# Reversed values copied in halves, key roots transposed later, one home for the triangular inverses of an RWKV-7 layer

## The chip, the cores and the metric

The kernel is one launch on one core of a Trainium2 chip. The metric is the device time of an execution in microseconds (us). A core has TensorE (PE, matrix products; its weight loads are shown as PEld), VectorE (DVE), ScalarE (ACT), GpSimd (POOL) and SyncE (SP, which issues nearly all DMAs here), which run their own instruction queues and wait for each other by semaphores. 16 DMA engines move data between DRAM and the on-chip memory (SBUF), and from DRAM to DRAM.

## The reference: one step of a four-layer backbone

The model has four layers over 640 tokens (128 of a context, 512 of a latent grid) and 1024 channels: retention, RWKV-7 time mixing, differential attention and neighbourhood attention. Each layer is a modulated norm, a mixer and an output product added to the residual stream. The change lies in the RWKV-7 layer and in what borders on it. Cut to what is computed there, for `x` the normed input:

```python
xx = centred_shift(h) - h
x_r, x_w, x_k, x_v, x_a, x_g = [h + xx * mu[n] for n in range(6)]
r, k, v, g = (x_r, x_k, x_v, x_g) @ w_in                 # 1024 x 4096
kk = k * k_k
kk = kk * rsqrt(max(sum(kk * kk, -1), 1e-12))            # per token and head of 64
for dr in range(2):                                      # forward, backward
    wlog  = -softplus(-(w0[dr] + tanh(x_w @ wA[dr]) @ wB[dr])) - 0.5
    decay = exp(-exp(wlog))
    a     = sigmoid(a0[dr] + (x_a @ aA[dr]) @ aB[dr])
    kd    = k * (1 + (a - 1) * k_a)
    seq   = (r, decay, kd, v, kk, a)                     # dr == 1: flipped in time
    # per token: s = s * decay + (s @ -kk) (kk * a)^T + v kd^T ;  y = s @ r
o = (head_layer_norm(y_f + y_b) + bonuses) * silu(g)
return o @ w_out
```

## The kernel before

**Numbers.** A product of two float32 matrices is made of three matmuls of rounded halves (lines 88, 89 and 90: high by high, low by high, high by low). ScalarE casts the high part (line 96 or 170), VectorE or GpSimd subtracts it for the low part (line 93). Weights come in pieces `wr` of 512 KB (line 160).

**Who sets the order.** The program is written with tiles that are taken from pools. A list scheduler with a timeline of its own orders the instructions of each engine by priority (`high_priority` raises it), and then lays the tiles out. A pool that is opened when another is closed gets the same addresses, so the first write to a tile waits until the last use of whatever lay there before. SyncE issues DMAs in one queue: a DMA that waits holds up all behind it.

**Stages.** Retention runs to about 586 us. Transition 0 is its output product (`ret_w_out`, 16 loads `wr`, matmuls `oa`), the residual, the norm of the next layer and its modulation (`w_mod`, matmuls `pm` on line 326); its rows of retention's output come back from DRAM as `oraw`. Then `rwkv_project` runs to about 1190, `rwkv_mix` to 1590, then transition 1 (`rwkv_w_out`) and the two attention layers.

**rwkv_project** mixes the shifted input (`wxh`, `wxl`: the parts of the mixed input `wm`) and projects it in the order k, the two low-rank ones, r, v, g, in column blocks `c2` of 256. The k part collects the squares of the keys per head in `wn` (line 1173), takes their roots on VectorE (lines 124 to 129, result `wny`), transposes them by TensorE (line 1189) and stores them to the DRAM tensor `wd_n`. The v part stores blocks `wvs` to `wd_v` (line 1150); the backward direction reads a copy `wd_vr` in which the two 64-column heads of a pair, and all others, stand in reversed column order. Woven in is `rwkv_prepare` for head pairs p = 0 to 7, which makes decays, keys and queries (`wBK`, `wQ`, `wLT`) and stores them to `wd_bk`, `wd_q`, `wd_lt` and `wd_lb`; it uses the low-rank second weights `wBr` (line 1230) and the normed keys `wkk` (line 1235).

**rwkv_inverse** (lines 1297 to 1318) inverts, for a pair p, 80 unit triangles of 32 x 32 that lie one per partition: it loads `wN` (line 1304), clears `wX` on GpSimd (line 1305), does 31 pairs of VectorE operations with a product `wtmp` (lines 1310 and 1312) and stores `wX` (line 1313) and its transposed copy (line 1316). Inverses 0 to 2 have their tiles in the project's pool `w1`, 3 to 7 in the mix's pool `w2`.

**rwkv_mix** loads for each p keys and queries `wKK` and `wBK` (lines 1412, 1413), the inverses `wTT` and `wTM`, the values `wUV` from `wd_v` and `wd_vr`, builds score blocks `wsc`, and runs `chain(p)`, the recurrence over chunks of 64 tokens (matmuls `wch`, lines 1507 and 1514, VectorE line 1518). `order2` gives the order in which the tiles of `w2` are first taken, hence their addresses.

Of the kernel before, what the change touches and what calls it, by code (L numbers as in the profile page):

```python
# [7 lines left out]
F32 = mybir.dt.float32  # L8
# [10 lines left out]
NP = 128  # L19
NS = 512  # L20
NT = 640
# [1021 lines left out]
NCH = 10  # L1043
# [29 lines left out]
class Rwkv:  # L1073
    def rwkv_project(s, hT, dr):

        nc, I = s.nc, s.I
        v, act, pe, gp = nc.vector, nc.scalar, nc.tensor, nc.gpsimd
        s.pj_bufs, s.wz_bufs = 3, 2
        with s.pool(name='w1', bufs=1) as w1, s.pool(name='w1p', bufs=1, space=PSUM) as pp:
# [1 line left out]
            T = lambda shape, name, bufs=1, dt=F32: w1.tile(shape, dt, name=name, tag=name, bufs=bufs)  # L1081
            xx = T([128, 8, NT], 'wxx')

            for k, shape in (('wN', [80, 32, 32]), ('wX', [80, 32, 32]), ('wBK', [128, NCH, 128]), ('wQ', [128, 2, NCH, 64]),
                             ('wLT', [128, NCH, 64]), ('wt1', [128, NT]), ('wt2', [128, NT]), ('wt4', [128, NT])):
                T(shape, k, s.pbufs.get(k, 1))
            for a, b in PARTS:
# [47 lines left out]
            for n, base, kind in ((2, 1024, 'k'), (0, 0, 'r'), (3, 2048, 'v'), (5, 3072, 'g')):  # L1135
                if kind == 'g' and s.rate:
                    s.fill_rest()
                x_ = mix(n, (0, HV, NT) if kind == 'k' else (0, NT))
                if prep is None:
                    s.tw = [T([128, NT], f'wtw{j}', 1, F32R) for j in range(2)]  # L1140
                    s.ta = [T([128, NT], f'wta{j}', 1, F32R) for j in range(2)]
                    prep = s.rwkv_prepare(w1, pp, dr)
                    next(prep)
                for c2 in range(4):
                    w = s.weights(W[:, base + c2 * 256:base + c2 * 256 + 256])
                    if kind == 'v':
                        for tt in range(5):
                            st = T([128, 256], 'wvs', 2)
                            act.copy(st, s.proj_N(w, tt, 256, x_))
                            nc.sync.dma_start(out=dr['v'][tt * 128:tt * 128 + 128, c2 * 256:c2 * 256 + 256], in_=st)  # L1150
                        step('v', c2)
                        continue
                    sts = [T([128, NT], 'wst', 2) for _ in range(2)]
                    if kind == 'k':
                        sqs = [T([128, NT], k) for k in ('wt1', 'wt2')]
                    for hf in range(2):
                        for cc in range(2):
                            c, st = c2 * 2 + cc, sts[cc]
                            ps = s.proj_T(w, cc, hf, x_)
                            sl = slice(hf * HV, hf * HV + HV)  # L1160
                            if kind == 'g':
                                th = T([128, HV], 'wth')
                                act.activation(out=th, in_=ps, func=AF.Tanh, scale=0.5)
                                v.scalar_tensor_tensor(out=st[:, sl], in0=th, scalar=1.0, in1=ps, op0=ALU.add, op1=ALU.mult)  # L1164
                            else:
                                act.copy(st[:, sl], ps)
                                if kind == 'k':
                                    act.activation(out=sqs[cc][:, sl], in_=ps, func=AF.Square, scale=s.vc('rwkv_kk', c))
                    for cc in range(2):
                        if kind == 'k':  # L1170
                            c = c2 * 2 + cc
                            for tt in range(5):
                                pe.matmul(nrm[:, 0, tt * 16:tt * 16 + 16], sqs[cc][:, tt * 128:tt * 128 + 128], s.ind[:, c, :], start=c + tt == 0, stop=c + tt == 11)
                        nc.sync.dma_start(out=dr[kind][c2 * 2 + cc], in_=sts[cc])
                    if kind in 'rg':
                        step(kind, c2)
                if kind == 'v':
                    for a, b in ((0, NP), (NP, NT)):
                        nc.sync.dma_start(out=dr['vr'][a:b].rearrange("t (a w) -> a t w", a=2),
                                          in_=dr['v'][a:b].rearrange("t (a w) -> a t w", a=2)[:, ::-1])  # L1180
                if kind == 'k':
                    n2, y_, t_ = (T([128, 80], k) for k in ('wn2', 'wny', 'wnt'))
                    v.tensor_scalar(out=n2, in0=nrm[:, 0, :80], scalar1=1e-12, scalar2=None, op0=ALU.max)
                    rn = s.rsqrt(w1, n2, None, None, y_, t_)
                    rt = T([128, NT], 'wst', 2)[:16]
                    for a, b in ((0, 4), (4, 5)):
                        ps = pp.tile([128, 512], F32, name='pj', tag='pj', bufs=s.pj_bufs)
                        for tt in range(a, b):
                            pe.transpose(ps[:16, (tt - a) * 128:(tt - a) * 128 + 128], rn[:, tt * 16:tt * 16 + 16], s.ident)
                        act.copy(rt[:, a * 128:b * 128], ps[:16, :(b - a) * 128])  # L1190
                    nc.sync.dma_start(out=dr['n'], in_=rt)
                    with s.tc.high_priority():
                        low_rank(1, I['rwkv_wA'][0], s.tw, AF.Tanh)
                        low_rank(4, I['rwkv_aA'][0], s.ta, AF.Copy)

    def rwkv_prepare(s, pool, pp, dr):

        nc, I = s.nc, s.I
# [22 lines left out]
        for p in range(8):  # L1221
# [70 lines left out]
                pe.matmul(pb[:, 2 * tt:2 * tt + 2], skd[:, tt * 128:tt * 128 + 128], s.ind[:, 0, 0:2], start=True, stop=True)  # L1292
            act.copy(s.cb[:, p, :], pb[:, :10])
            if p not in s.inv_late:
                s.rwkv_inverse(T, dr, p)
            yield

    def rwkv_inverse(s, T, dr, p):

        nc = s.nc  # L1300
        gp = nc.gpsimd
        v = gp if p in s.inv_pool else nc.vector
        N_, X_ = T([80, 32, 32], 'wN'), T([80, 32, 32], 'wX')
        nc.sync.dma_start(out=N_, in_=dr['lt'][p].rearrange("b i u s t -> (b i u) s t"))
        gp.memset(X_, 0.0)
        gp.memset(X_.rearrange("p s t -> p (s t)")[:, ::33], 1.0)
        for j in range(31):
            n = 31 - j
            t = T([80, 256], 'wtmp', s.tmp_bufs)[:, :(j + 1) * n].rearrange("p (s t) -> p s t", t=n)
            v.tensor_tensor(out=t, in0=X_[:, 0:j + 1, j:j + 1].to_broadcast([80, j + 1, n]),  # L1310
                            in1=N_[:, j:j + 1, j + 1:].to_broadcast([80, j + 1, n]), op=ALU.mult)
            v.tensor_tensor(out=X_[:, 0:j + 1, j + 1:], in0=X_[:, 0:j + 1, j + 1:], in1=t, op=ALU.subtract)  # L1312
        nc.sync.dma_start(out=dr['tt'][p].rearrange("b i u s t -> (b i u) s t"), in_=X_)
        Q_ = N_[0:40]
        nc.scalar.copy(Q_, X_[0:40].rearrange("p s t -> p t s"))
        nc.sync.dma_start(out=dr['tq'][p].rearrange("i u s t -> (i u) s t"), in_=Q_)
# [15 lines left out]
    def rwkv_mix(s, dr, od):  # L1332
# [4 lines left out]
        with s.pool('w2') as w2, s.pool('w2p', space=PSUM) as pp:  # L1337
            T = lambda shape, name, bufs=1, dt=F32: w2.tile(shape, dt, name=name, tag=name, bufs=bufs)
            P = lambda name, bufs, shape=(128, 512): pp.tile(list(shape), F32, name=name, tag=name, bufs=bufs)
            z = lambda shape, name, dt=F32: w2.tile(shape, dt, name=name)  # L1340
            inverse = lambda p: p in s.inv_late and s.rwkv_inverse(T, dr, p)

            u64, u128 = [128, 2, 20, 64], [128, 2 * NCH, 128]
            bt, rr, qa = [128, NCH, 128], [128, 2, NCH, 2, 64], [128, 2 * NCH, 2, 64]
# [301 lines left out]
class Run:  # L1646
    def run(s):
        nc, tc, I = s.nc, s.tc, s.I
        with tc.tile_pool(name='pc', bufs=1) as pc, tc.tile_pool(name='pd', bufs=1, space=DRAM) as pd:
# [52 lines left out]
            with s.pool('plr') as plr:  # L1702
                s.wc = plr.tile([128, 8, 20], F32, name='wwc')
                s.wcn = plr.tile([128, 8, 2, 10], F32, name='wwcn')
                s.cb = plr.tile([128, 8, 10], F32, name='wcb')
                s.ind = plr.tile([128, 8, 16], F32, name='ind')
                nc.sync.dma_start(out=s.ind, in_=I['rwkv_ind'])
                ph = s.pool('phw', side=RIGHT)
                hT = ph.tile([128, 8, NT], F32, name='hT')
                s.w_bufs, s.wr_bufs = 5, 2  # L1710
                with s.pool('px0', side=RIGHT) as pr, s.weight_pool(bufs=1), s.pool('po0') as po:

                    s.touch_weights()
                    rhs = s.load_out(po, od, 16, right=pr)
                    x = pr.tile([128, 8, NT], F32, name='x0r')
                    reload(0, x)
                    s.transition(x, I['ret_w_out'][0], 16, rhs, 0, [[0], [1], [2], [3]], (hT,))
                    store(1, x)
                s.w_bufs, s.wr_bufs = 3, s.rwkv_wr
                s.fill_with(s.todo_rwkv, s.rwkv_rate if s.todo_rwkv else 0)  # L1720
                od = s.rwkv(lambda: ph.__exit__(None, None, None), hT)
# [50 lines left out]
class Kernel(Net, Ret, Rwkv, Diff, Na, Run):  # L1772
    hp = (600, 1, 1, 1, 300, 0, 0)
    preps = {'r': (2, 2, 2, 2)}
    bkv = 12
    order2 = ('KK', 'BK', 'RR1', 'QT', 'QA1', 'BT00', 'UV0', 'BT10', 'RS0', 'BT01', 'BT11', 'R01', 'RS1', 'R10', 'UV1', 'R11', 'TT1', 'QA0', 'RR0', 'R00', 'misc', 'pad448', 'vt', 'sg')
    todo_ret = [(0, 4), (0, 5), (1, 0), (1, 1), (1, 2), (1, 3), (1, 4), (1, 5)]
    todo_rwkv = []
    todo_t = {0: [(2, 0), (2, 1), (2, 2), (2, 3), (2, 4), (2, 5)], 1: [(3, 0), (3, 1), (3, 2), (3, 3), (3, 4), (3, 5)]}
# [66 lines left out]
```

## Time and profile before

| | us |
|---|---|
| median of 3 runs | 2610.86 (2610.16 to 2616.23) |
| profiled execution | 2608.0 |
| its span, first to last instruction | 2606.2 |
| TensorE busy | 2308.8 |
| VectorE busy | 1500.5 |
| ScalarE busy | 1067.3 |
| GpSimd busy | 675.5 |
| mean granted TensorE clock | 0.925 of full speed |

The profiled execution is one more run of the same kernel. The span leaves out 1.8 us around the first and last instruction. Shares of busy time are means over stages that have different limits, so the stages have to be looked at one by one, and in each the row of the engine that stands: what it waited for, and what stood ahead of that in its own queue.

### The profile page before, as it was taken

What the parts mean: (1) busy time and instruction counts of PE and PEld (TensorE: products, weight loads), DVE (VectorE), ACT (ScalarE), POOL (GpSimd) and SP (SyncE); (2) the same over time, 40 slices, a digit from 0 to 9 for tenths busy, and PEclk for the clock granted to TensorE, in tenths of its full rate; (3) what the DMA queues carried; (4) which work ended last, traced back from release to release, by engine and by line L of the source; (5) the groups of instructions that cost most, each with busy time, mean ns of one, the idle gap of its engine ahead of it and who ended that gap; (6) DMA issues with size and microseconds to landing.
All of it is one profiled execution on the core that took longest, in us unless ns stands there. A gap on an engine that the chain in (4) does not pass through costs nothing.

```text
span 2606.2 us, 48698 instructions
## 1 busy us (share of the span) xinstructions
PE 2308.8 (89%) x18951; PEld 2086.3 (80%) x18951; DVE 1500.5 (58%) x3511; ACT 1067.3 (41%) x2405; POOL 675.5 (26%) x576
## 2 busy tenths in 40 slices
PE   7999999997988999294888997889889888999998
PEld 5888888987958889194777877688888887898888
DVE  7534343443173898394888554657776665645554
ACT  5323233332153655152333342245554433645551
POOL 3323232303210000001243433233222323332321
PEclk9999999998988889695888888899999998999999
DMA  8433333225272566367365645511111122223321
GB/s 294 131 101 102 118 101 110 90 85 188 83 262 69 166 191 216 107 193 182 102 148 136 160 126 177 175 56 48 45 55 39 51 68 56 67 76 78 77 71 57
DMA packets 344586, 303.54 MB, mean 116 GB/s; under 512 B 140220, under 2 KB 281044, under 8 KB 344356
## 3 DMA queue, kind: packets, MB, share of 16 engines
q1 hardware_dynamic: 344356, 300.44, 38.8%
q8 instruction: 149, 2.44, 0.4%
q14 instruction: 81, 0.66, 0.1%
HBM read 231.37 MB, written 64.79 MB: 114 GB/s over the span
## 4 chain that ended last, share of the span: by engine, by line
PE 34%; DVE 14%; DMA 4%; issue 3%; ACT 3%; SPq 3%; POOL 1%; ACTq 0%; DVEq 0%; POOLq 0%
PE pj L88 5%; PE pj L89 5%; PE pj L90 5%; PE oa L88 2%; PE oa L89 2%; PE oa L90 2%; DVE wtmp L1310 2%; DVE wX L1312 1%; PE nO L1024 1%; PE wsc L1439 1%; PE dtp L839 1%; PE wch L1507 1%; PE npt L1007 1%; PE wy L1541 1%; SPq L160 1%
## 5 line engine op out<-in xcount | busy, mean ns | idle before, releaser
L93 POOL TENSOR_TENSOR wl<-wr,wh 128x1024 fp32r<-128x1024 f32 (+1 forms) x168 | 371.2, 2222 | 628.5 <-ACT wh L170 490.4
L88 PE MATMUL pj<-hH,wh 128*128 128x320 f32 x1280 | 408.2, 321 | 10.5 <-ACT hH L96 7.1
L89 PE MATMUL pj<-hL,wh 128*128 128x320 f32 x1280 | 406.7, 318 | 3.0 <-POOL hL L93 2.4
L90 PE MATMUL pj<-hH,wl 128*128 128x320 f32 x1280 | 404.1, 316 | 0.1
L88 PEld LDWEIGHTS pj<-hH,wh 128*128 128x128 f32 x1280 | 246.4, 193 | 24.3 <-ACT hH L96 10.4
L89 PEld LDWEIGHTS pj<-hL,wh 128*128 128x128 f32 x1280 | 247.1, 193 | 10.6 <-POOL hL L93 3.8
L90 PEld LDWEIGHTS pj<-hH,wl 128*128 128x128 f32 x1280 | 246.5, 193 | 2.4 <-issue 1.0
L170 ACT CAST wh<-wr 128x1024 fp32r<-128x1024 f32 x168 | 175.5, 1047 | 133.7 <-PE pj L89 48.6
L88 PE MATMUL oa<-oh,wh 128*128 128x384 f32 (+1 forms) x640 | 201.6, 316 | 20.6 <-ACT wh L170 14.4
L89 PE MATMUL oa<-ol,wh 128*128 128x256 f32 (+1 forms) x640 | 199.3, 313 | 0.1
L88 PE MATMUL pj<-wh,hH 128*128 128x256 f32 x640 | 188.4, 294 | 12.2 <-DVE dr L756 7.4
L90 PE MATMUL oa<-oh,wl 128*128 128x256 f32 (+1 forms) x640 | 199.1, 312 | 0.0
L89 PE MATMUL pj<-wl,hH 128*128 128x256 f32 x640 | 186.0, 291 | 0.0
L90 PE MATMUL pj<-wh,hL 128*128 128x256 f32 x640 | 185.4, 290 | 0.0
L88 PE MATMUL pj<-wxh,wh 128*128 128x320 f32 x416 | 132.8, 327 | 53.2 <-DVE wst L1164 44.8
L88 PEld LDWEIGHTS pj<-wh,hH 128*128 128x128 f32 x640 | 127.5, 199 | 20.3 <-DVE dr L756 8.3
L88 PEld LDWEIGHTS oa<-oh,wh 128*128 128x128 f32 x640 | 122.8, 192 | 23.7 <-ACT wh L170 16.3
L89 PE MATMUL pj<-wxl,wh 128*128 128x320 f32 x416 | 134.5, 325 | 2.2 <-DVE wxl L93 2.2
L90 PE MATMUL pj<-wxh,wl 128*128 128x320 f32 x416 | 133.8, 323 | 1.9 <-DVE wl L93 1.9
L88 PEld LDWEIGHTS pj<-wxh,wh 128*128 128x128 f32 x416 | 82.1, 199 | 58.1 <-DVE wst L1164 45.1
L89 PEld LDWEIGHTS pj<-wl,hH 128*128 128x128 f32 x640 | 127.7, 200 | 0.0
L90 PEld LDWEIGHTS pj<-wh,hL 128*128 128x128 f32 x640 | 127.5, 199 | 0.0
(479 smaller groups left out, 5601.0 us busy)
## 6 DMA issues: line engine op xcount, KB each, us to landing
wr<-in_ret_w_in SPq DMA_DIRECT2D x48, 512.0 KB
wm<-in_w_mod SPq DMA_DIRECT2D x40, 512.0 KB
wr<-in_w_mod SPq DMA_DIRECT2D x32, 512.0 KB
wr<-in_rwkv_w_in SPq DMA_DIRECT2D x32, 512.0 KB
wl<-in_w_mod SPq DMA_DIRECT2D x24, 512.0 KB
wr<-in_diff_w_in SPq DMA_DIRECT2D x48, 256.0 KB
wr<-in_na_w_in SPq DMA_DIRECT2D x48, 256.0 KB
wd_bk<-wBK SPq DMA_DIRECT2D x16, 640.0 KB
```

Source lines behind the costliest of these rows:

```text
L88: mm(out, l[0], r[0], start=start, stop=False)
L89: mm(out, l[0], r[1], start=False, stop=False)
L90: mm(out, l[1], r[0], start=False, stop=stop)
L93: eng.tensor_tensor(out=lo, in0=src, in1=hi.bitcast(F32), op=ALU.subtract)
L160: nc.sync.dma_start(out=raw[:, :, c:c + x.shape[1]], in_=x[j * 128:(j + 4) * 128].rearrange("(k p) c -> p k c", p=128))
L170: nc.scalar.copy(hi[:, :, :n], raw[:, :, :n])
L839: pe.matmul(po, at[:, j * 128:j * 128 + 128], v_[:, vt, cc * 128:cc * 128 + 128], start=j == 0, stop=j == nt - 1)
L1007: pe.transpose(pt[:, j * 128:j * 128 + 128], P[:, j * 128:j * 128 + 128], s.ident)
L1024: pe.matmul(ot_ps[i * 64:i * 64 + 64, oc:oc + 128], vt[j][:, hc:hc + 64], pts[i][:, j * 128:j * 128 + 128], start=j == 0, stop=j == len(vt ...
L1310: v.tensor_tensor(out=t, in0=X_[:, 0:j + 1, j:j + 1].to_broadcast([80, j + 1, n]), in1=N_[:, j:j + 1, j + 1:].to_broadcast([80, j + 1, n]) ...
L1312: v.tensor_tensor(out=X_[:, 0:j + 1, j + 1:], in0=X_[:, 0:j + 1, j + 1:], in1=t, op=ALU.subtract)
L1439: pe.matmul(ps[:, u - u0, :], QT[:, u, :], TT[:, u, :], start=True, stop=True)
```

## The change

There are five edits.

- **Values reversed in halves.** In place of two copies after the whole v part (tokens 0 to 127 and 128 to 639, each in two blocks of 512 columns), two copies follow after every second column block, each in eight blocks of 64 columns.
- **Roots' transposes later.** The five transposes of the key norms, their two copies and the store of `wd_n` stand behind the first low-rank projection in the program text.
- **One home for the inverses' tiles.** `wN`, `wX` and `wtmp` are taken from the pool `plr`, which lives through the whole RWKV layer, with one buffer each.
- **Keys' tiles elsewhere.** 'KK' and 'BK' move from the first place of `order2` to the place behind 'TT1'.
- **A smaller scratch area.** `dynamic_dma_scratch_size=1024` is passed to the builder; tiles on the left side of SBUF lie 15,360 bytes lower in each partition during retention.

```diff
@@ rwkv_project
-            for k, shape in (('wN', [80, 32, 32]), ('wX', [80, 32, 32]), ('wBK', [128, NCH, 128]), ('wQ', [128, 2, NCH, 64]),
+            for k, shape in (('wBK', [128, NCH, 128]), ('wQ', [128, 2, NCH, 64]),
...
+                        if c2 % 2:
+
+                            hc = slice(c2 // 2 * 512, c2 // 2 * 512 + 512)
+                            for a, b in ((0, NP), (NP, NT)):
+                                blocks = [dr[k][a:b, hc].rearrange("t (a w) -> a t w", a=8) for k in ('vr', 'v')]
+                                nc.sync.dma_start(out=blocks[0], in_=blocks[1][:, ::-1])
                         step('v', c2)
...
-                if kind == 'v':
-                    for a, b in ((0, NP), (NP, NT)):
-                        nc.sync.dma_start(out=dr['vr'][a:b].rearrange("t (a w) -> a t w", a=2),
-                                          in_=dr['v'][a:b].rearrange("t (a w) -> a t w", a=2)[:, ::-1])
                 if kind == 'k':
...
-                    rt = T([128, NT], 'wst', 2)[:16]
-                    for a, b in ((0, 4), (4, 5)):
...
-                    nc.sync.dma_start(out=dr['n'], in_=rt)
                     with s.tc.high_priority():
                         low_rank(1, I['rwkv_wA'][0], s.tw, AF.Tanh)
+                        rt = T([128, NT], 'wst', 2)[:16]
+                        for a, b in ((0, 4), (4, 5)):
+                            ps = pp.tile([128, 512], F32, name='pj', tag='pj', bufs=s.pj_bufs)
+                            for tt in range(a, b):
+                                pe.transpose(ps[:16, (tt - a) * 128:(tt - a) * 128 + 128], rn[:, tt * 16:tt * 16 + 16], s.ident)
+                            act.copy(rt[:, a * 128:b * 128], ps[:16, :(b - a) * 128])
+                        nc.sync.dma_start(out=dr['n'], in_=rt)
                         low_rank(4, I['rwkv_aA'][0], s.ta, AF.Copy)
@@ rwkv_inverse
+        T = lambda shape, name, bufs=1: s.pinv.tile(shape, F32, name=name, tag=name, bufs=bufs)
@@ build
+                s.pinv = plr
+                for k, sh, n in (('wN', [80, 32, 32], 1), ('wX', [80, 32, 32], 1), ('wtmp', [80, 256], s.tmp_bufs)):
+                    plr.tile(sh, F32, name=k, tag=k, bufs=n)
@@ class Kernel
-    order2 = ('KK', 'BK', 'RR1', 'QT', ... 'R11', 'TT1', 'QA0', ...)
+    order2 = ('RR1', 'QT', ... 'R11', 'TT1', 'KK', 'BK', 'QA0', ...)
@@ main
-    nc = bacc.Bacc("TRN2", target_bir_lowering=False, num_devices=1)
+    nc = bacc.Bacc("TRN2", target_bir_lowering=False, num_devices=1, dynamic_dma_scratch_size=1024)
```

The order of instructions changes on all engines. Three places on SyncE's queue follow, of before and then of the changed kernel; a row gives the line, the operation, its output and input, and the shape.

The end of the v part, before. `wd_vr` is the reversed copy, `wr` a piece of the weights, `wBr` the low-rank second weight:

```order
L1150 DMA wd_v<-wvs 128x256 x3
L160 DMA wr<-in_rwkv_w_in 128x4x256
L1179 DMA wd_vr<-wd_v 2x512x512
L160 DMA wr<-in_rwkv_w_in 128x4x256
L1271 DMA wd_q_7671<-wQ 128x2x640
L1230 DMA wBr<-in_rwkv_aB 128x128
```

And in the changed kernel:

```order
L1150 DMA wd_v<-wvs 128x256 x2
L1156 DMA wd_vr<-wd_v 8x128x64
L1150 DMA wd_v<-wvs 128x256 x2
L160 DMA wr<-in_rwkv_w_in 128x4x256
L1156 DMA wd_vr<-wd_v 8x512x64
L160 DMA wr<-in_rwkv_w_in 128x4x256
L1273 DMA wd_q_7683<-wQ 128x2x640
L1232 DMA wBr<-in_rwkv_aB 128x128
```

The copy has the same neighbours as before; it is that of the second half, in smaller pieces. The first half's copies stand some 25 and 50 rows ahead.

The end of retention, before. `oraw` is retention's output read back, `x0r` the residual, `wr` the output weights:

```order
L648 DMA rs_5657<-in_state_ret 64x512 x2
L1633 DMA oraw<-ret_od 128x640 x8
L683 DMA ret_od<-rot 128x640 x2
L1664 DMA x0r<-xd_64 128x640 x3
L683 DMA ret_od<-rot 128x640
L1664 DMA x0r<-xd_64 128x640
L1633 DMA oraw<-ret_od 128x640
L1664 DMA x0r<-xd_64 128x640
L1633 DMA oraw<-ret_od 128x640
L1664 DMA x0r<-xd_64 128x640 x2
L683 DMA ret_od<-rot 128x640
L160 DMA wr<-in_ret_w_out 128x4x256 x2
```

And in the changed kernel:

```order
L160 DMA wr<-in_ret_w_out 128x4x256 x2
L648 DMA rs_5580<-in_state_ret 64x512
L640 DMA out_state_ret<-rs_5574 64x512 x2
L648 DMA rs_5657<-in_state_ret 64x512 x2
L1636 DMA oraw<-ret_od 128x640 x3
L160 DMA wr<-in_ret_w_out 128x4x256
L1636 DMA oraw<-ret_od 128x640
L160 DMA wr<-in_ret_w_out 128x4x256
L1636 DMA oraw<-ret_od 128x640 x2
L160 DMA wr<-in_ret_w_out 128x4x256 x2
L683 DMA ret_od<-rot 128x640
L160 DMA wr<-in_ret_w_out 128x4x256
```

The loads of the output weights stand ahead of and between the reads of retention's output, where they stood behind nearly all of them.

The start of the mix, before. The numbers behind `wd_tt`, `wd_tq`, `wd_q` and `wd_bk` are those of the DRAM tensors of one pair each; `wd_q_7666` is pair 0, `wd_tt_7700` the inverse of pair 2:

```order
L1384 DMA wTM<-wd_tq_7707 32x20x32
L1313 DMA wd_tt_7700<-wX 80x1024
L1384 DMA wTM<-wd_tq_7707 32x20x32
L1316 DMA wd_tq_7708<-wN 40x1024
L1388 DMA wTT_12388<-wd_tt_7699 32x20x32
L1413 DMA wBK<-wd_bk_7674 128x1280
L1412 DMA wKK<-wd_q_7666 128x640 x2
L1413 DMA wBK<-wd_bk_7674 128x1280
```

And in the changed kernel, where `wd_q_7678` is pair 0, `wd_tt_7712` the inverse of pair 2 and `wd_lt_7697` the input of inverse 3:

```order
L1289 DMA wd_lb_7709<-wLT 32x10x32
L1415 DMA wKK<-wd_q_7678 128x640
L1418 DMA wR_12400<-wd_q_7678 64x10x64
L1415 DMA wKK<-wd_q_7678 128x640
L1316 DMA wd_tt_7712<-wX 80x1024
L1319 DMA wd_tq_7720<-wN 40x1024
L1416 DMA wBK<-wd_bk_7687 128x1280
L1307 DMA wN<-wd_lt_7697 80x1024
```

The loads of `wKK` stand ahead of the stores of inverse 2, and those of `wBK` of pair 0 are gone from here (they stand some 200 rows ahead); the load of `wN` for inverse 3, which stood some 80 rows ahead of these stores, stands behind them.

## Rows read from the trace of the kernel before

**Rows 1.** The page: busy time, share of span, instructions.

```profile
PE 2308.8 (89%) x18951; PEld 2086.3 (80%) x18951; DVE 1500.5 (58%) x3511; ACT 1067.3 (41%) x2405; POOL 675.5 (26%) x576
```

**Rows 2.** Windows: stretch, length, busy times, clock, DMA share, GB/s.

```profile
590.00:602.00 12.00, 0.71 (x2) 0.71 (x3) 3.48 (x5) 3.52 (x5) 0.69 (x1) 0.50 1.05 392
602.00:610.00 8.00, 8.00 (x36) 7.75 (x36) 4.63 (x3) 3.63 (x5) 4.61 (x2) 0.72 0.65 221
...
1061.00:1102.00 41.00, 0.36 (x3) 0.09 (x1) 2.49 (x7) 3.16 (x10) 0.00 (x0) 0.54 0.32 100
1102.00:1190.00 88.00, 74.01 (x710) 69.50 (x711) 81.17 (x191) 42.44 (x95) 10.25 (x11) 0.87 0.66 197
1190.00:1209.00 19.00, 0.93 (x41) 0.86 (x42) 4.03 (x15) 3.01 (x5) 2.23 (x1) 0.50 0.74 193
...
1240.00:1574.00 334.00, 296.69 (x5003) 255.35 (x5005) 235.68 (x630) 122.92 (x288) 125.24 (x214) 0.88 0.52 133
```

**Rows 3.** Time line of SyncE's queue: start, duration, engine, line, DMA.

```profile
1051.04 0.61 SPq L1179 DMA_DIRECT2D wd_vr<-wd_v  x1
1051.75 33.14 SPq L160 DMA_DIRECT2D wr<-in_rwkv_w_in  x1
1084.99 4.62 SPq L1271 DMA_DIRECT2D wd_q<-wQ  x1
1089.70 1.19 SPq L1230 DMA_DIRECT2D wBr<-in_rwkv_aB  x1
```

**Rows 4.** Time line of VectorE: in brackets idle before, and releaser.

```profile
1049.77 0.82 DVE L93 TENSOR_TENSOR wxl<-wm,wxh 128x640 fp32r<-128x640 f32 x1 [4.96 <-ACT wxh L96]
...
1099.09 0.61 DVE L93 TENSOR_TENSOR wB<-wBr,wB 64x128 fp32r<-64x128 f32 x2 [38.20 <-ACT wB L1232]
```

**Rows 5.** DMA from 1065 to 1083: packets, then share of 16 engines.

```profile
DMA packets 450, 0.92 MB, mean 51 GB/s; under 512 B 0, under 2 KB 0, under 8 KB 450
...
q1 hardware_dynamic: 450, 0.92, 13.1%
```

**Rows 6.** DMA from 1190 to 1201: the same.

```profile
DMA packets 4221, 1.44 MB, mean 131 GB/s; under 512 B 4078, under 2 KB 4078, under 8 KB 4221
...
q1 hardware_dynamic: 4221, 1.44, 60.1%
```

**Rows 7.** Time line of SyncE's queue at transition 0.

```profile
592.96 1.22 SPq L160 DMA_DIRECT2D wr<-in_ret_w_out  x2
```

**Rows 8.** Waits of TensorE, 586 to 612: us, times, longest.

```profile
PE oa L88 <- ACT wh L170: 14.4, 1, 14.4
```

**Rows 9.** Windows of tile wxh: PE, PEld, DVE, ACT; then as above.

```profile
735.00:767.00 32.00, 11.90 (x44) 8.34 (x44) 8.28 (x17) 8.65 (x18) 0.95 0.82 284
```

**Rows 10.** Time line of TensorE at the roots.

```profile
836.14 1.23 PE L1189 MATMUL pj<-ident,wny 128*16 128x128 f32 x5 [11.57 <-DVE wny L129]
...
837.98 0.47 PE L88 MATMUL pj<-wxh,wh 128*128 128x320 f32 x1
```

**Rows 11.** Time line of TensorE at the start of the mix.

```profile
1208.82 1.30 PE L1422 MATMUL wtp<-ident,wKK 128*128 128x128 f32 x5 [18.04 <-DMA wKK<-wd_q]
...
1231.74 1.26 PE L1471 MATMUL wtp<-ident,wBK 128*128 128x128 f32 x4 [6.23 <-POOL wBK L1465]
```

**Rows 12.** Time line of SyncE's queue at the start of the mix.

```profile
1198.46 0.45 SPq L1313 DMA_DIRECT2D wd_tt<-wX  x1
...
1203.23 0.91 SPq L1412 DMA_DIRECT2D wKK<-wd_q  x2
...
1225.28 1.04 SPq L1313 DMA_DIRECT2D wd_tt<-wX  x1
```

**Rows 13.** Lines 1313 and 1312: count, ns, first and last start.

```profile
L1313 SPq DMA_DIRECT2D wd_tt<-wX x8: 318/358/1150, 980.7 to 1445.4; - x8
L1312 DVE TENSOR_TENSOR wX<-wX,wtmp x248: 163/365/1611, 913.5 to 1437.9; 80x31 f32<-80x31 f32 x8, 80x87 f32<-80x87 f32 x8, 80x135 f32<-80x135 f32 x8, 80x175 f32<-80x175 f32 x8
```

**Rows 14.** Waits of SyncE's queue, 1570 to 1595.

```profile
SPq L160 <- POOL wyc L1567: 7.3, 1, 7.3
```

More of the change, by code (lines that the diff above doesn't have):

```diff
@@ L1184, in rwkv_project @@
                     rn = s.rsqrt(w1, n2, None, None, y_, t_)
-                    rt = T([128, NT], 'wst', 2)[:16]
-                    for a, b in ((0, 4), (4, 5)):
[L1187 to L1190, printed above, removed]
-                    nc.sync.dma_start(out=dr['n'], in_=rt)
                     with s.tc.high_priority():
                         low_rank(1, I['rwkv_wA'][0], s.tw, AF.Tanh)
+                        rt = T([128, NT], 'wst', 2)[:16]
[5 more added lines that the diff above has]
+                        nc.sync.dma_start(out=dr['n'], in_=rt)
                         low_rank(4, I['rwkv_aA'][0], s.ta, AF.Copy)
@@ L1294, in rwkv_prepare, with rwkv_inverse @@
             if p not in s.inv_late:
-                s.rwkv_inverse(T, dr, p)
+                s.rwkv_inverse(dr, p)
             yield
-    def rwkv_inverse(s, T, dr, p):
+    def rwkv_inverse(s, dr, p):
         nc = s.nc
@@ L1340, in rwkv_mix @@
             z = lambda shape, name, dt=F32: w2.tile(shape, dt, name=name)
-            inverse = lambda p: p in s.inv_late and s.rwkv_inverse(T, dr, p)
+            inverse = lambda p: p in s.inv_late and s.rwkv_inverse(dr, p)
             u64, u128 = [128, 2, 20, 64], [128, 2 * NCH, 128]
@@ L1775 @@
     bkv = 12
-    order2 = ('KK', 'BK', 'RR1', 'QT', 'QA1', 'BT00', 'UV0', 'BT10', 'RS0', 'BT01', 'BT11', 'R01', 'RS1', 'R10', 'UV1', 'R11', 'TT1', 'QA0', 'RR0', 'R00', 'misc', 'pad448', 'vt', 'sg')
+    order2 = ('RR1', 'QT', 'QA1', 'BT00', 'UV0', 'BT10', 'RS0', 'BT01', 'BT11', 'R01', 'RS1', 'R10', 'UV1', 'R11', 'TT1', 'KK', 'BK', 'QA0', 'RR0', 'R00', 'misc', 'pad448', 'vt', 'sg')
     todo_ret = [(0, 4), (0, 5), (1, 0), (1, 1), (1, 2), (1, 3), (1, 4), (1, 5)]
```

## The prediction, made before the changed kernel was timed

> **What bounds the kernel now.** I read the busy line of the page first, then the windows by stage, then the waits and time lines of the stages in which TensorE stands. TensorE is busy 89% of the span [rows 1], so a gain can only come from the few places where it stands, and the windows show where: it works 0.71 of 12 us ahead of transition 0, 0.36 of 41 us at the end of the value projection and 0.93 of 19 us ahead of the mix [rows 2]. Its clock is at 0.50 to 0.54 of full speed in these stretches, and 0.72 in the 8 us after the first: a stall also makes the matmuls behind it slower. In the mix itself TensorE is busy 297 of 334 us and is the bound [rows 2]; between 1102 and 1190 VectorE is (81 of 88 us, TensorE 74).
>
> The profiled execution took 2608.0 us with a span of 2606.2; the 1.8 us around the span stay. It lies 2.9 us below the median of 2610.86, so I subtract from 2608.0 and add 2.9 at the end.
>
> **A. The reversed copy of v, in halves.** The two old copies go DRAM to DRAM in two blocks of 512 columns, so in pieces of 2 KB. While the second runs, 450 packets of 0.92 MB take 13.1% of 16 engines over 18 us [rows 5]: that is 2.1 engines and 18 x 16 x 0.131 / 450 = 84 ns a piece. The 512-token copy has 1024 pieces, 512 on each of the two, so T = 43 us. SyncE issues it at 1051.04; the next issue, a weight load, holds SyncE's queue for 33.14 us, a store of wQ 4.62 us more, and only then, at 1089.70, goes the load of the small low-rank weight wBr [rows 3] for which VectorE stands 38.20 us, to 1099.09 [rows 4]. The 128-token copy ahead of it has T = 128 x 84 ns = 10.8 us and shows 4.96 us of VectorE idle [rows 4]. Both fit idle = T - 5: the 5 us is work that was still in hand.
>
> New, each half (512 of 1024 columns) is copied as soon as its four column blocks of v are stored, in eight blocks of 64 columns: pieces of 256 B, eight times as many for the same bytes. I take eight engines, since two blocks occupied two. Per half: 512 pieces an engine for the 512 tokens, 128 for the others. The trace has no small DRAM-to-DRAM piece. The nearest row is loads and stores that are small on one side: 4221 packets, 4078 of them under 512 B, take 60.1% of 16 engines over 11 us [rows 6], 25 ns each; with 143 large ones at some 110 ns taken off, 22 ns. At 22 ns T is 11.3 us and 2.8 us, the idle 6.3 us per half and none, 12.6 in all: against 43.2 that is a gain of 31. Ends: 10.5 ns (bytes alone, 256/2048 of 84) leaves only 0.4 us per half, a gain of 42; 84 ns a piece whatever its size makes 2 x 38 + 2 x 5.8 = 88 us, a loss of 44. I take 22 ns, the nearest row. What is late next: VectorE's own work, since it is 92% busy in the 88 us behind the stall.
>
> The Trainium skill (DMA: Bandwidth & Descriptors, Specifications) says that transfers reach line rate from 512 B up and that below this the engine reads, modifies and writes. This speaks against the change. By it a 256 B piece would cost two passes of 512 B, an estimate of twice 21 ns from the 2 KB row, 42 ns. The rows of small packets, at 22 to 25 ns, don't bear it out, but none of them writes DRAM from DRAM; by that rule the gain of A is 10 in place of 31, and it is a rival below.
>
> **B. Transition 0.** TensorE waits 14.4 us for the first cast of the output weights [rows 8]. SyncE issues the second pair of these loads at 592.96 [rows 7], when retention's last tiles free the place. The diff's last line (a smaller scratch area, so that all tiles lie 15,360 B lower) changes which tiles share addresses: the order now has 6 of the loads ahead of or between the reads of retention's outputs, so matmuls are ready when the projection ends. Ends: 0 (the other loads and the last outputs are still late), and 14.4 plus 8 x 0.28 of lost clock, 17. I take 12.
>
> **C. Start of the k projection.** The same shift puts the first tile of wxh on tiles that the modulation weights hold until their last matmul; in the order the k projection now follows all of them. Of the k projection TensorE does 11.9 us between 735 and 767 [rows 9], which would move behind. The cover is the modulation's own loads, which keep DMA 0.82 busy there, and VectorE. Ends: nothing, and a loss of 12. I take a loss of 4.
>
> **D. The roots.** The five transposes of the key norms stand in TensorE's queue ahead of the low-rank projection, and wait 11.57 us for VectorE's rsqrt; the matmuls behind them then take 0.47 us, the half-clock length [rows 10]. Moved behind low_rank(1), that projection and its wz product fill the wait. The same DMA, and the load of wkk behind it, come later by the length of that projection, but VectorE's queue has some 25 operations of the first preparation ahead of its use. Ends: nothing, and 11.6 plus about 2 of clock. I take a gain of 8.
>
> **E. Start of the mix.** The first KK and BK lay over wN and wX of the preparation: those of wKK are issued at 1203.23, behind the stores of inverse 2 at 1198.46 [rows 12], and TensorE stands 18.04 us until 1208.82 for wKK; then 6.23 us for GpSimd's first product with wBK [rows 11], whose queue was held by the clearing of wX for inverse 4. With KK and BK behind 'TT1' in the region, both BK loads go during the projection and KK ahead of those stores. Ends: nothing (RR and UV loads are as late), and 24. I take 12.
>
> **F. One home for all inverses.** wN, wX and wtmp now have one buffer each. Before, inverse 3 had its own tiles in the mix's pool and ran beside inverse 2; now it begins when 2 has left, near chain(0). This takes 62 operations of about 0.365 us [rows 13], 22 us, out of the stretch where VectorE is the bound: there TensorE's 74 of 88 us [rows 2] caps the gain at 14, and I take 6. In return five inverses, not four, run in series under the mix. Four take 1445.4 - 1225.28 = 220 us [rows 12, 13], 55 each: five need 275, and with some 48 us for the last products and chain 323, while the mix lasts 334 for TensorE alone. Hidden, but by 11 us: I take a loss of 6. Net 0, ends -14 and +38 (five at 66 us, a fifth longer than the four took: 330 + 48 is 44 over the 334, less the 6).
>
> **G. Transition 1.** The second buffer of its weights comes to lie over tiles of the last finish, and its load, which waited 7.3 us for GpSimd [rows 14], goes behind the store of that finish's result. Ends 0 and +7; I take +3.
>
> Sum: -31 - 12 + 4 - 8 - 12 + 0 + 3 = -56. 2608.0 - 56 = 2552, and 2.9 for the median: 2555. Every engine's order is laid out anew by the scheduler; I allow 10 us either way for that.
>
> **The rivals.** (1) Small pieces cost twice their bytes: A gives 10 in place of 31, 2576. For it: a copy that both reads and writes small pieces in DRAM is in no row. Against: 22 ns in [rows 6]. (2) The inverses bound the mix: at 66 us each F is +38, 2593. For it: the margin is 11 us, each inverse waits for its store, its load and VectorE. It decides from (334 - 48) / 5 = 57 us an inverse on, against 55 measured. (3) The other side: each piece costs what a large one does, 84 ns. The stall then comes twice, A is +44, the sum -25 + 44 = +19, 2630. All other gains are used up from 69 ns a piece on (A = +25). Against it are the rows of small packets, for it only that DRAM to DRAM is not among them. (4) The waits come back in other names: B, D and E each find another load as late, A gives 20, C and G cost as said: -13, 2598, or with the small pieces at 42 ns no change.
>
> **Chances.** My forecast 0.50 (its own range 2535 to 2572), rival 1 0.12, rival 2 0.15, rival 4 0.13 with a half of it within the bound, rival 3 0.07, something unnamed 0.03. A run of this kernel can tell 0.3%, about 8 us. So faster 0.84, same 0.08, slower 0.08. The range that leaves out rival 3 and half of the outer tails: 2526 to 2604.
>
> **What would show it.** After: VectorE's idle in front of wB some 6 us, the copies' packets 256 B at about 22 ns on 8 engines; no 14 us wait of TensorE for the output weights; no 11 us wait at the roots' transposes; KK waits under 6 us; five inverses whose last store comes some 48 us or more before the last chain ends. I am wrong if VectorE still stands 20 us or more behind a copy, or if TensorE in the mix waits for products of an inverse.

## The result and the profile after

The changed kernel takes 2582.31 us (median of 4, 2579.8 to 2586.9) against 2610.98 for the kernel before (median of 4): 28.7 us less, a ratio of 0.9888 with a 95% interval of 0.9868 to 0.9908. It is faster by 1.1%, by half of the 56 us that I had added up; 2555 was forecast. That is inside the stated range of 2526 to 2604 and outside the 2535 to 2572 of the forecast alone. The profiled execution is the 2586.9 us one, with a span of 2585.1, the longest of the four.

One sentence ahead of the prediction is wrong: `wd_vr` is `wd_v` with its tokens in reversed order, not its columns. The sizes of the copy's pieces are not touched by that.

The busy line of the changed kernel's page, which answers to [rows 1]:

```profile
PE 2323.3 (90%) x18951; PEld 2088.9 (81%) x18951; DVE 1497.6 (58%) x3511; ACT 1068.6 (41%) x2405; POOL 671.9 (26%) x576
```

TensorE is busy 14.5 us longer with the same number of instructions. The windows of the changed kernel answer to [rows 2], with the mix taken from its first chain matmul to its last:

```profile
590.00:602.00 12.00, 9.75 (x62) 8.66 (x61) 4.71 (x8) 3.47 (x5) 1.54 (x3) 1.00 0.81 285
1061.00:1102.00 41.00, 34.13 (x280) 31.89 (x281) 29.90 (x61) 25.02 (x55) 1.11 (x2) 0.92 0.72 202
1102.00:1139.00 37.00, 33.67 (x301) 32.31 (x300) 34.43 (x64) 17.14 (x40) 8.49 (x8) 1.00 0.66 202
1170.00:1544.00 374.00, 305.49 (x4893) 261.58 (x4894) 249.43 (x697) 123.10 (x284) 127.28 (x216) 0.82 0.50 124
```

The empty stretches ahead of transition 0 and at the end of the value projection are filled, at a clock of 0.92 to 1.00 where it was 0.50 to 0.54. But the mix takes 374 us, where it took 330, and its granted clock is 0.82 where it was 0.88 [rows 2].

A table of five places in the traces shows where time is gained and given back. It has the end of the last matmul `oa` of transition 0 and of the last projection matmul, the start of the first transpose of `wKK`, the start of the first and end of the last chain matmul (line 1507 before), the difference of these two, and the span; all in us, and all kernels of the experiments:

| kernel | T0 end | project end | wKK | chain first | chain last | mix | span | median (ratio to before, interval) |
|---|---|---|---|---|---|---|---|---|
| before | 718 | 1175 | 1209 | 1241 | 1570 | 330 | 2606.2 | |
| after | 711 | 1134 | 1148 | 1170 | 1543 | 374 | 2585.1 | 2582.3 (0.9888, 0.9868 to 0.9908) |
| e1 two homes | 704 | 1128 | 1141 | 1179 | 1518 | 338 | 2552.7 | 2554.4 (0.9799, 0.9775 to 0.9822) |
| e2 two wN | 704 | 1128 | 1141 | 1169 | 1520 | 350 | 2548.1 | 2547.4 (0.9772, 0.9752 to 0.9791) |
| e3 old homes | 719 | 1133 | 1147 | 1173 | 1562 | 389 | 2604.3 | 2604.0 (0.9987, 0.9969 to 1.0005) |
| e4 inverse 3 early | 708 | 1131 | 1145 | 1173 | 1530 | 356 | 2565.6 | 2566.2 (0.9846, 0.9825 to 0.9867) |
| e5 copy alone | 719 | 1136 | 1175 | 1208 | 1536 | 328 | 2568.0 | 2565.9 (0.9835, 0.9802 to 0.9868) |
| e6 scratch alone | 719 | 1173 | 1195 | 1214 | 1596 | 383 | 2624.5 | 2626.3 (1.0066, 1.0039 to 1.0094) |
| e7 roots alone | 717 | 1156 | 1203 | 1233 | 1562 | 329 | 2596.5 | 2598.8 (0.9959, 0.9943 to 0.9976) |
| e8 home and order | 708 | 1163 | 1178 | 1202 | 1586 | 384 | 2609.3 | 2613.9 (1.0019, 1.0002 to 1.0036) |
| e9 copy and roots | 718 | 1134 | 1174 | 1207 | 1537 | 330 | 2573.0 | 2573.8 (0.9870, 0.9849 to 0.9892) |
| e10 copy in 8 blocks | 718 | 1146 | 1179 | 1210 | 1543 | 333 | 2575.8 | 2579.9 (0.9891, 0.9864 to 0.9917) |
| e11 two wN, early 3 | 708 | 1132 | 1145 | 1172 | 1517 | 344 | 2543.0 | 2544.9 (0.9756, 0.9732 to 0.9779) |
| e12 two wN, old places | 705 | 1126 | 1142 | 1170 | 1515 | 345 | 2545.3 | 2543.9 (0.9751, 0.9722 to 0.9781) |

The experiments ran on other occasions than the changed kernel, beside 7 to 20 runs of the kernel before with medians of 2606 to 2609; they are compared by their ratios, of which 0.001 is 2.6 us.

At its first chain matmul the changed kernel is 71 us ahead of the kernel before: the terms that act until then came to 65 in my sum (31 + 12 - 4 + 8 + 12, and 6 of F). At its last one it is 27 ahead. What went wrong lies in the mix.

**The copy.** SyncE's queue at the second half's copy, to be held against [rows 3], and VectorE's first product with `wB`, against [rows 4]:

```profile
1045.63 0.68 SPq L1156 DMA_DIRECT2D wd_vr<-wd_v  x1
1046.40 8.55 SPq L160 DMA_DIRECT2D wr<-in_rwkv_w_in  x1
1055.00 0.50 SPq L1273 DMA_DIRECT2D wd_q<-wQ  x1
1055.55 0.47 SPq L1232 DMA_DIRECT2D wBr<-in_rwkv_aB  x1
```

```profile
1061.34 0.28 DVE L93 TENSOR_TENSOR wB<-wBr,wB 64x128 fp32r<-64x128 f32 x1 [2.36 <-ACT wB L1234]
```

The weight load behind the copy holds the queue 8.55 us in place of 33.14, and VectorE stands 2.36 us in place of 38.20. The first half's copy, from 1010 to 1016, in the same view as [rows 5]:

```profile
DMA packets 3230, 0.83 MB, mean 138 GB/s; under 512 B 3230, under 2 KB 3230, under 8 KB 3230
...
q1 hardware_dynamic: 3230, 0.83, 60.4%
```

All packets are small ones: 6 x 16 x 0.604 / 3230 = 18 ns each, and 138 GB/s where the old copy moved 51 [rows 5]. A half's 1.31 MB takes 9.5 us.

**The inverses.** SyncE's queue in the changed kernel: the store of one inverse (line 1316), and the load for the next (line 1307). The first pair are inverses 2 and 3:

```profile
1148.25 0.54 SPq L1316 DMA_DIRECT2D wd_tt<-wX  x1
...
1191.06 0.42 SPq L1307 DMA_DIRECT2D wN<-wd_lt  x1
...
1237.90 0.32 SPq L1316 DMA_DIRECT2D wd_tt<-wX  x1
...
1250.32 0.50 SPq L1307 DMA_DIRECT2D wN<-wd_lt  x1
...
1302.62 0.34 SPq L1316 DMA_DIRECT2D wd_tt<-wX  x1
...
1474.12 0.61 SPq L1316 DMA_DIRECT2D wd_tt<-wX  x1
```

Inverse 3, which was stored at 1225.28 before [rows 12], 15 us ahead of the first chain matmul, is now loaded 43 us behind the store of inverse 2 and 21 us behind that matmul. From there five follow one another until 1474.12. The last chain ends 69 us later. Between the store of inverse 2 and the load for inverse 3 SyncE issues 56 other DMAs, which the list ahead of the prediction leaves out.

TensorE now waits for what the inverses give. The first row is its wait for `wTM`, the transposed inverses, from 1150 to 1565; the kernel before has no such row in its mix. The others are the last of these waits, for inverse 7, and the first matmul of the last chain:

```profile
PE wtp L1399 <- DMA wTM<-wd_tq: 8.6, 3, 4.7
```

```profile
1484.84 0.71 PE L1399 MATMUL wtp<-wTM,wLB 32*32 32x32 f32 x34 [4.67 <-DMA wTM<-wd_tq]
...
1516.25 0.33 PE L1510 MATMUL wch<-wRS,wQA 128*64 128x64 f32 x2
```

These direct waits are only a part of the 44 us by which the mix is longer. Between the first and the last chain matmul TensorE is also busy 305 us in place of 292, at the lower clock, and it stands 8.23 us for `wBK`, where the longest such wait of the kernel before is 0.9:

```profile
1180.31 0.45 PE L1432 MATMUL wsc<-wBK,wKK 64*64 64x64 f32 x2 [8.23 <-DMA wBK<-wd_bk]
```

### The profile page after: what moved, and what is told of

Its sections match the earlier page's. It is cut to its first block, busy times and chain, and to the rows that moved or that the text cites. A ratio compares the mean times of both kernels' runs of the same rounds, so it can differ in the third digit from the quotient of the medians.

```text
span 2585.1 us, 48681 instructions
## 1 busy us (share of the span) xinstructions
PE 2323.3 (90%) x18951; PEld 2088.9 (81%) x18951; DVE 1497.6 (58%) x3511; ACT 1068.6 (41%) x2405; POOL 671.9 (26%) x576
## 4 chain that ended last, share of the span: by engine, by line
PE 62%; DVE 16%; DMA 9%; ACT 5%; issue 4%; SPq 2%; POOL 1%; ACTq 0%; DVEq 0%; POOLq 0%
PE pj L88 11%; PE pj L89 11%; PE pj L90 11%; PE oa L88 3%; PE oa L89 3%; PE oa L90 3%; PE pm L326 2%; PE wsc L1442 2%; DVE wtmp L1313 1%; DVE wX L1315 1%; PE nO L1024 1%; PE ro L90 1%; PE ro L88 1%; PE ro L89 1%; PE dtp L839 1%
## 5 line engine op out<-in xcount | busy, mean ns | idle before, releaser
L89 PEld LDWEIGHTS pj<-hL,wh 128*128 128x128 f32 x1280 | 244.6, 191 | 11.9 <-POOL hL L93 5.0
L89 PEld LDWEIGHTS oa<-ol,wh 128*128 128x128 f32 x640 | 122.8, 192 | 2.5 <-DVE ol L93 2.3
```

What stands on the lines that cost most here:

```text
L89: mm(out, l[0], r[1], start=False, stop=False)
```

## The experiments

**The homes of the inverses, changed on the changed kernel.** In e1 both tiles get two buffers, in e2 `wN` alone, in e3 the old homes come back, in e4 inverse 3 is called in the preparation.

```diff
 e1 -('wN', [80, 32, 32], 1), ('wX', [80, 32, 32], 1)
    +('wN', [80, 32, 32], 2), ('wX', [80, 32, 32], 2)
 e2 -('wN', [80, 32, 32], 1)
    +('wN', [80, 32, 32], 2)
 e3 -        T = lambda shape, name, bufs=1: s.pinv.tile(...)
    +    def rwkv_inverse(s, T, dr, p):     # wN, wX, wtmp in w1 and w2 again
 e4 -    inv_late = (3, 4, 5, 6, 7)
    +    inv_late = (4, 5, 6, 7)
```

> The changed kernel with two buffers each for wN and wX instead of one. Theory: the mix lasts 374 us instead of 330 because the inverses follow each other in one home; with two, inverse 3 runs during the projection again and the next load lies under the inverse before: the mix comes back to 325 to 340 us, the time to 2535 to 2550. Rival 1 (VectorE's queue in the mix is what stretches each inverse, whatever the home): 2575 to 2585. Rival 2 (the new place of KK and BK stretches the mix): no gain either, 2575 to 2585.

> The changed kernel with two buffers for wN alone; wX keeps one. Theory (serial home): the 12 to 17 us from the store of one inverse to the first operation of the next shrink by the load's part, some 8 us for each of five, but inverse 3 still waits for wX of inverse 2: 2545 to 2565. Rivals 1 and 2: 2575 to 2585.

> The changed kernel with the inverses' tiles where they were, in the pools of the projection and of the mix; scratch size, order2, copy and roots as changed. In its order of SyncE the load for inverse 3 still stands behind the stores of inverse 2. Theory (what counts is when inverse 3 can start, not the pool's name): about as the changed kernel, 2570 to 2590. Rival (the move into the long-lived pool itself costs): 2535 to 2550.

> The changed kernel with inverse 3 called during the preparation instead of the mix (inv_late from 4 on), one home as changed. Theory: inverse 3 starts some 12 us behind the store of 2, so 30 us earlier than the 1191 us at which it is loaded now, and four are left under the mix: the mix gets back 25 to 40 of its 44 us, 2545 to 2560. Rival 1 (VectorE): VectorE has room in the projection now, so a gain of 22 us of VectorE work at most out of the mix, 2560 to 2580.

Measured: e1 2554.4, e2 2547.4, e3 2604.0 and e4 2566.2. By the ratios e1, e2 and e4 are 23, 30 and 11 us faster than the changed kernel, and e3 is 26 us slower. The store of line 1316 in e1 and in e2, with the first and last start:

```profile
L1316 SPq DMA_DIRECT2D wd_tt<-wX x8: 373/512/1287, 994.8 to 1378.3; - x8
```

```profile
L1316 SPq DMA_DIRECT2D wd_tt<-wX x8: 319/332/639, 988.5 to 1407.9; - x8
```

The last inverse is stored 96 and 66 us earlier than in the changed kernel, the mix takes 338 and 350 us in place of 374, and TensorE has no wait for `wTM` in either. So the late series of inverses is shown to be what stretched the mix, and a second `wN` is enough to end it. e1 came in 4 us above the theory's range, e2 inside it; both lie far below the two rivals. At the end of the last chain they are 26 and 24 us ahead of the changed kernel; what they gain behind it I didn't look into. The mix isn't quite back at 330: with the inverses done 110 to 140 us before the last chain ends, something else holds the rest. In e2 6.21 us of it are again a wait for `wBK`:

```profile
1177.63 0.44 PE L1432 MATMUL wsc<-wBK,wKK 64*64 64x64 f32 x2 [6.21 <-DMA wBK<-wd_bk]
```

VectorE, which in e2 works on inverse 3 until 25 us behind the first chain matmul, is a further candidate that I didn't test.

e4's inverse 3 is loaded 6 us behind the store of 2:

```profile
1144.98 0.54 SPq L1316 DMA_DIRECT2D wd_tt<-wX  x1
1151.16 0.54 SPq L1307 DMA_DIRECT2D wN<-wd_lt  x1
1199.55 0.32 SPq L1316 DMA_DIRECT2D wd_tt<-wX  x1
```

It stores it 38 us earlier than the changed kernel, but its last inverse, at 1460.73, only 13 us: the loads for inverses 6 and 7 go 25 and 22 us behind the stores before them, where they went 11. The mix is shorter by 18 us, less than the 25 to 40 that I expected, and 2566.2 us lie in the range of rival 1, VectorE. The trace is for the theory: TensorE still waits 7.9 us for `wTM`, and the last chain ends 69 us behind the last store, as in the changed kernel.

e3 missed its interval on the slow side. Its pools have their old names, yet its queue is that of the changed kernel:

```profile
1147.20 0.54 SPq L1315 DMA_DIRECT2D wd_tt<-wX  x1
...
1195.54 0.42 SPq L1306 DMA_DIRECT2D wN<-wd_lt  x1
...
1245.37 0.37 SPq L1315 DMA_DIRECT2D wd_tt<-wX  x1
```

Inverse 3 is loaded 48 us behind the store of 2, and its mix is the longest of all. It isn't the pool that decides, but whether the load for inverse 3 goes ahead of that store. The traces of all fourteen kernels agree. In the five in which it goes behind (the changed kernel, e3, e4, and e6 and e8 below), the mix takes 356 to 389 us, TensorE waits 5.8 to 8.6 us for `wTM`, and the last two chains start 40 to 47 us behind the stores of their own inverses. In the other nine the mix takes 328 to 350 us, there is no such wait, and no chain starts less than 64 us behind its store.

And transition 0, which ends at 711 in the changed kernel, ends at 719 here as before, although the scratch area is the small one.

**The parts alone, on the kernel before.**

```diff
 e5 +  if c2 % 2: two copies of 512 columns, a=8          (and the copies behind v taken out)
 e6 +  dynamic_dma_scratch_size=1024
 e7 +  rt, the five transposes and the store of dr['n'] behind low_rank(1)
 e8 +  s.pinv = plr, one buffer each; order2 with 'KK', 'BK' behind 'TT1'
```

> The kernel before with the reversed copy in halves and eight blocks, nothing else changed. Theory (each part's term holds by itself): VectorE's 38 us in front of wB fall to some 3 to 8 us, -30 to -38, 2570 to 2580 against 2607. Rival (the stall ends elsewhere, since the start of the mix waits for inverses 2 and 3): inverse 3 cannot end earlier by as much, -15 to -25.

> The kernel before with the smaller scratch area alone. My prediction put the early loads of the output weights down to it: TensorE's 14.4 us before transition 0 go, -8 to -15. Rival (it takes the scratch area and the 10 KB of the new home together to bring the weights onto other addresses, since the kernel with the old homes and the smaller area still began its output product at 602 us): no change, within 5 us.

> The kernel before with the roots' transposes behind the first low-rank projection, nothing else changed. Theory: TensorE's 11.6 us before the transposes fall to about 4, -6 to -9 at the end of the projection. Rival (it is given back: the keys' norms come 10 us later, so the first preparation and the inverses behind it come no earlier, and the mix is gated by these): within 3 us.

> The kernel before with the one home of the inverses' tiles and the new place of KK and BK; copy, roots and scratch size as before. Theory (serial home): the mix starts 10 to 20 us earlier and lasts 40 us longer: 20 to 30 us slower, 2625 to 2640. Rival (the gains at the start outweigh it): 2595 to 2607.

e5 is 43 us faster than the kernel before in the medians and 38 in the spans, more than the 30 to 38 expected. VectorE's waits for `wB` are 2.8 us in all. So one of the five edits gives at least as much as all of them (0.9835 against 0.9888; the intervals touch at 0.9868). The start of the mix isn't helped beyond the copy: TensorE still waits for `wKK`,

```profile
1174.82 1.30 PE L1424 MATMUL wtp<-ident,wKK 128*128 128x128 f32 x5 [23.00 <-DMA wKK<-wd_q]
```

e6 is 17 us slower. TensorE's waits at transition 0, in the view of [rows 8], and SyncE's queue at inverses 2 and 3:

```profile
PE oa L88 <- ACT wh L170: 14.6, 1, 14.6
```

```profile
1185.69 1.04 SPq L1313 DMA_DIRECT2D wd_tt<-wX  x1
...
1239.77 0.42 SPq L1304 DMA_DIRECT2D wN<-wd_lt  x1
```

The wait at transition 0 is the old one, as its rival said, so my reason for term B is wrong. The rival's time, within 5 us, is missed too: the scratch area alone puts the load for inverse 3 54 us behind the store of inverse 2 and stretches the mix to 383 us, which none of my theories had. Why this shift of addresses sets the load so late I didn't find out.

e7 gains 10 us, a little more than expected. TensorE's wait for the roots falls from 11.57 to 4.3 us:

```profile
PE pj L1191 <- DVE wny L129: 4.3, 1, 4.3
```

e8 is about as fast as the kernel before (0.2% slower), between its theory and its rival. Its first chain matmul is 38 us earlier, its mix 54 us longer. Its wait at transition 0 is gone, with the scratch area as before:

```profile
PE oa L88 <- ACT oh L96: 3.0, 2, 2.1
```

So the scratch area isn't needed for it, against e6's rival too. e12 below has lost the wait with the old places of 'KK' and 'BK', and e3, which has all edits but the home, keeps 14.8 us of it: it is the home, 10 KB in each partition, that ends the wait. That it does so by bringing the output weights onto free addresses is my reading and not shown.

**The copy's form, the sum of two parts, and two mends.**

```diff
 e9  = e5 and e7 together
 e10 -  rearrange("t (a w) -> a t w", a=2)        (before, both copies behind v)
     +  rearrange("t (a w) -> a t w", a=8)
 e11 = e2 with inv_late = (4, 5, 6, 7)
 e12 = e2 with order2 as before, 'KK' and 'BK' first
```

> The kernel before with the two edits that gained alone, the copy in halves and the later transposes; homes, places of KK and BK and scratch size as before. Theory (the two gains add, and the other three edits of the change together cost what the one home takes from the mix): -43 - 10, 2550 to 2562, some 25 us under the changed kernel. Rival (the copy's gain is only whole with the roots early): 2565 or more.

> The kernel before with its copies still behind the whole v part, but in eight blocks of 128 columns (512 B pieces, eight engines) in place of two. Theory (the number of engines ends the stall): 512 pieces an engine at some 20 to 30 ns are 10 to 15 us instead of 43, VectorE waits 5 to 10 us, -28 to -38 against the kernel before. Rival (it is the halves, half of the bytes out of the way early, that end it): -10 to -20.

> The changed kernel with two buffers for wN and inverse 3 called during the preparation, the two mends together. Theory: with two wN inverse 3 already ran during the projection, so the early call adds nothing: 2542 to 2552. Rival (the inverses still gate the last pairs): 2530 to 2540.

> The changed kernel with two buffers for wN and the old order of first tiles in the mix, KK and BK in front. Theory (the new place of KK and BK gives its gain at the start of the mix only by moving them off the inverses' tiles, which the home does too, so the old place is as good): 2542 to 2555. Rival (in front they come to lie over other tiles of the preparation that are used to its end): the mix starts 10 to 15 us later, 2555 to 2565.

e9 takes 2573.8: the two gains don't add. Both e5 and e9 end the projection at 1134 to 1136 and start the chain at 1207 to 1208, and both last chains end at 1536 to 1537. With the copy mended, the roots' 10 us are given back before the projection ends. The 5 us between the two spans arise behind the mix, in layers that are the same in both, so I don't count them. The rival's wording (2565 or more) holds, not its reason.

e10 gains 28 us of e5's 43 with eight blocks alone. SyncE's queue, VectorE's wait, and the packets from 1050 to 1061:

```profile
1048.79 0.66 SPq L1179 DMA_DIRECT2D wd_vr<-wd_v  x1
1049.55 12.38 SPq L160 DMA_DIRECT2D wr<-in_rwkv_w_in  x1
```

```profile
1068.89 0.61 DVE L93 TENSOR_TENSOR wB<-wBr,wB 64x128 fp32r<-64x128 f32 x2 [10.25 <-ACT wB L1232]
```

```profile
DMA packets 3490, 1.87 MB, mean 170 GB/s; under 512 B 15, under 2 KB 3489, under 8 KB 3489
...
q1 hardware_dynamic: 3489, 1.87, 56.1%
```

The 512 tokens' 2.1 MB take 12.3 us at 170 GB/s, as long as the queue is held. The packets take 56.1% of 16 engines where the copy in two blocks took 13.1% [rows 5]. So the eight blocks, by what looks like more engines at work, do most of it, at the weak end of the theory's range. The other 15 us come with the halves, which have smaller pieces too; the intervals of e5 and e10 just touch.

e11 and e12 are the fastest kernels run, 2544.9 and 2543.9: 2.4% and 2.5% under the kernel before, and by the ratios 34 and 36 us faster than the changed kernel. As expected the early call adds nothing that can be told from e2, and the old places of 'KK' and 'BK' are as good as the new ones once the home is long-lived and has two `wN`.

## Why the prediction was half right

The direction, and the range, held; the likeliest time did not. Up to the first chain matmul the gain is 71 us where the terms came to 65, the mix costs 44 where F had 6, and what is behind it costs 6 where G had 3: 21 us of span, where I had 56. That the first of these three came out near its sum is partly luck, since A and E are larger than I had them, C costs more, and D gives nothing that can be seen beside the copy. By its steps:

**A, the copy, 31 us forecast.** The mechanism is right and the size was too small: alone it gives 38 us of span (e5). A piece takes 18 ns, not 22, and the second half's idle is 2.4 us where idle = T - 5 gave 6.3. The trace before had this number: of the packets in [rows 6], 2304 are of 256 B and take 17.5 ns on the mean; I had taken off the 143 large ones at 110 ns each, where they take some 300. The rivals of 42 and 84 ns a piece are out. The Trainium skill (DMA: Bandwidth & Descriptors, Why small descriptors are slow) gives a 256 B descriptor a fixed overhead of 27%. The traces show 138 GB/s with 256 B and 170 GB/s with 512 B pieces, a fifth less, which is nearer to that than to the halving that I derived from the same page's line rate rule.

**B and C, transition 0 and the k projection, a gain of 12 and a loss of 4.** Transition 0 ends 7.6 us earlier in the changed kernel, 10.5 in e8. The reason given, the scratch area, is wrong: e6 has it and keeps the wait, e8 has the home without it and loses the wait. The k projection's loss is some 10 us, near the bound of 12 that I had: TensorE's projection work between 735 and 767 is 8.8 us, where [rows 9] show 11.9, and e8, which gains 10.5 at the end of transition 0, is level with the kernel before a fifth of the way through its projection. Together B and C are about nothing in the changed kernel.

**D, the roots, 8 us.** The wait went as described (4.3 us remain) and e7 gains 10 us by it alone. In company it is worth nothing that e9 shows.

**E, the start of the mix, 12 us.** Right, and too small: TensorE waits 2.89 us for `wKK` where [rows 11] show 18.04,

```profile
1148.05 1.08 PE L1425 MATMUL wtp<-ident,wKK 128*128 128x128 f32 x4 [2.89 <-DMA wKK<-wd_q]
```

and between the projection's end and the first chain matmul lie 35 us in place of 66. The new places of 'KK' and 'BK' are one way to it and not the only one: e12 has the old places and the home, e3 the new places and the old homes, and both come to `wKK` 14 to 16 us behind the projection's end, where it was 34.

**F, one home, net 0. This is the step that failed.** I had five inverses of 55 us start with the mix and 48 us of products and chain behind them: 323 us, hidden under 334. The five take 283 us (1191.06 to 1474.12), 57 each, so the pace was nearly right. The start and the tail were not. The first is loaded 21 us after the first chain matmul, since in SyncE's order 56 DMAs stand between the store of inverse 2 and its load. And what follows the last store takes 69 us, not 48: 42 until the last chain's first matmul at 1516.25, and 27 for that chain. 21 + 283 + 69 = 373, the mix's length. Both could have been read: the place of that load in the queue's order, and the chains in the trace before, which start 44 us apart on the mean and of which the last takes 23, 67 together.

TensorE's waits for `wTM`, 8.6 us, are the sign of being wrong that I had named. The other sign, a last store 48 us or more before the last chain ends, is met with 69 us and told nothing, since the products and the chain behind the store need more than that. It is the mechanism of rival 2, which I gave 0.15, for another reason than the slower inverses that I gave it; e1 and e2 show it by taking it away, e4 by taking away a part, and e6 and e8 by bringing it in without the rest.

**G, transition 1, a loss of 3.** From the last chain to the middle of transition 1's output product the lead shrinks from 27 to 16 us, of which 3.52 us are a new wait of TensorE for the first weights:

```profile
1571.31 0.69 PE L88 MATMUL oa<-oh,wh 128*128 128x384 f32 x1 [3.52 <-ACT wh L170]
```

At the end it is 21 again. I didn't test this part.

That the terms may be added was a step as well, and e9 speaks against it: two parts that act on the same stretch, the projection up to its last preparation, gave the larger of the two and not the sum.

## What to carry to other kernels

A tile that loses its second copy can turn parallel work into a series; count the series from where the order really starts it to the end of everything that needs its last member, and hold that against the stage that should hide it. An edit that moves addresses can set such a wait (here the scratch size alone, e6, and the home with the new places, e8), so each is to be run alone. A DRAM-to-DRAM copy is to be cut into more blocks first (e10: 28 of the 43 us), and a large one is worth a look at what stands behind it in the same queue.

## What the runs showed of the hardware

A DRAM-to-DRAM copy in two blocks moves 51 GB/s with 2 KB pieces; in eight blocks it moves 170 GB/s with 512 B and 138 GB/s with 256 B pieces. If eight engines work, that is 21 and 17 GB/s an engine against 25: eight times smaller pieces cost a third of an engine's rate, and four times the engines return far more. The number eight is my reading of the eight blocks and not shown: the packets' shares of 56.1% and 60.4% of 16 engines would be 9.0 and 9.7. A packet's mean time in these three stretches is 84 ns for 2 KB, 27.5 for 512 B and 17.9 for 256 B. I had not expected small pieces that are both read from and written to DRAM to be this cheap. And a load issued behind such a copy holds its queue for about as long as the copy lasts: 33.14 us of 41 (2.1 MB at 51 GB/s), 12.38 of 12.3 and 8.55 of 7.6 (1.05 MB at 138 GB/s).
